# Weight buffers spaced by 64 bytes, one pair of x tiles shifted by 32, and a single mask tile in a hybrid attention layer

## The chip, the cores and the metric

The kernel runs on one core of one Trainium2 chip. The metric is the device time of one execution in microseconds. The unchanged kernel takes 2168.59 us (median of two runs, 2168.49 and 2168.7).

## What is computed

The reference is one decoder layer on 2048 tokens of width 1024, with 16 learned meta tokens ahead of them. Everything is float32. The input is normalised, multiplied by one wide matrix, and the product is cut into ten pieces:

```python
xn = rms_norm(h, norm_gain[l])
proj = xn @ w_in[l]
sb_q, sb_k, sb_v, sw_q, sw_k, sw_v, sb_z, sw_z, g_sb, g_sw = jnp.split(proj, offsets, axis=-1)
o_sb = stick_breaking_attention(sb_q, sb_k, sb_v, valid)            # 8 heads of 64, causal
o_sw = sliding_window_sink_attention(rope(sw_q), rope(sw_k), sw_v, attn_sinks[l], valid)
                                                                    # 16 heads, 2 kv heads, window 128
y_sb = (o_sb * jax.nn.silu(sb_z)) @ w_branch_sb[l]
y_sw = (o_sw * jax.nn.silu(sw_z)) @ w_branch_swa[l]
merged = jax.nn.sigmoid(g_sb) * y_sb + jax.nn.sigmoid(g_sw) * y_sw
h = h + merged @ w_out[l]
return rms_norm(h, final_norm_gain)[:, BLOCK:]
```

## The kernel before

Nearly all arithmetic is matrix products on TensorE. To keep float32 accuracy in the faster float32r format, every operand is split into a high and a low part (`wh`, `wl` for weights, `xh`, `xl` for activations), and a product is three matmuls: high by high, high weights by low activations, low weights by high activations. The first operand below, `lhsT`, is the weight tile of 128x128 that is loaded into the array; the second, `rhs`, is the moving tile of 128x512 that is streamed through it. Lines 403 to 405 are the projection loop, run for each column tile of `w_in` and each of four groups of 512 tokens:

```python
for k in range(KT):                                                     # KT = 8
    T.matmul(acc, lhsT=wh[:, k, :], rhs=xh[g][:, k, :], ...)            # L403
    T.matmul(acc, lhsT=wh[:, k, :], rhs=xl[g][:, k, :], ...)            # L404
    T.matmul(acc, lhsT=wl[:, k, :], rhs=xh[g][:, k, :], ...)            # L405
```

While one matmul streams, the weights of the next one are loaded; a matmul and its weight load are shown apart in the profile (PE and PEld).

The order of the program, in time:

1. A start, in which the first tiles of x are prepared. Here two groups are also multiplied in an unnormalised form, from tiles `uh` and `ul` instead of `xh` and `xl`.
2. Two halves of the sequence, groups 2 and 3 first, then 0 and 1. In each half, projections are woven with sliding-window attention (its matmuls are lines 698, 727, 744), then with stick-breaking attention (lines 841, 863, 889), by a generator that puts a few projection matmuls between pieces of attention. Between and after these come stretches of projections alone, the gate tiles (`gate`, made by `tiles_by_tile`).
3. The end (`finish`): the two branch projections (`project`, lines 223 to 225, with `wh` and `wl` against ring tiles `ringl` or `ringr`) and the output projection (lines 282 to 284, in which `ringl` is loaded as the weights and `ringr` streams).

TensorE's order is written out by hand (`manual_schedule`), so it follows the code; the other engines are ordered by a scheduler, except in the start.

What matters for this change is where tiles lie in a partition of SBUF. `weights` (line 163) takes `wh` and `wl` from pool `w`, three buffers each, 4096 bytes per partition and buffer: 8 blocks of 128 float32. `x_tiles` (line 371) takes pairs `xh`, `xl` of 16384 bytes each from pool `x`, one pair for each of two groups. The ring tiles are 2048 bytes each; two unused tiles, `padl` of 672 bytes (line 189) and `padr` of 1728 bytes (line 243), lie ahead of them. The start addresses in the built program, modulo 512 bytes, are:

| tiles | address modulo 512 |
|---|---|
| `wh`, `wl`, all six buffers | 480 |
| `xh`, `xl`, both pairs | 480 |
| `ringl`, `ringr` | 480 |
| `uh`, `ul` | 320 |

"Distance" in this text is the address of the moving tile of one matmul minus the address of the weights that are loaded while it streams, that is, those of the next matmul, modulo 512. A block of `wh`, `wl`, or of `xh`, `xl`, a ring tile and a slice of 128 columns are all multiples of 512 bytes, so the distance is a property of the pair of tiles: 0 between `xh` or `xl` and any weight buffer, 0 between the ring tiles and the weights and among the ring tiles, 352 between `uh` or `ul` and the weights. Among attention matmuls it takes various values (256 and 384 in line 744, 384 and 448 inside a pair of line 841, 256 and 224 for the low part `wtl` of line 889).

The mask `sel` (line 68) holds two equal copies of a 128x128 pattern, loaded by two DMAs in `late_consts`; line 702 uses it as the predicate of a copy into the scores of two heads.

Of the kernel before, what the change touches and what calls it, by code (L numbers as in the profile page):

```python
# [7 lines left out]
F32 = mybir.dt.float32  # L8
F32R = mybir.dt.float32r
I32 = mybir.dt.int32  # L10
# [6 lines left out]
P = 128  # L17
D = 1024
KT = D // P
# [25 lines left out]
def tile_kernel(ctx, tc, x, xt, meta, metat, gain, w_in, w_sb, w_sw, w_out, sinks, fgain,  # L45
# [6 lines left out]
    V, A, G, T = nc.vector, nc.scalar, nc.gpsimd, nc.tensor  # L52

    def DMA(dst, src):
        nc.sync.dma_start(*(t.bitcast(F32) if t.dtype == F32R else t for t in (dst, src)))

    ctx.enter_context(tc.manual_schedule(engines={mybir.EngineType.PE}))
    cp = ctx.enter_context(tc.tile_pool(name="const", bufs=1, side="left"))
# [3 lines left out]
    def ps(tag):  # L62
        return pp.tile([P, 512], F32, tag=tag, name="ps_" + tag, bufs={"g": 2, "z": 2, "zm": 1, "t": 2, "o": 1}[tag])
# [1 line left out]
    A.preload_act_table_set("natural_log_exp_and_others")  # L65
    ident = cp.tile([P, P], F32, name="ident")
    gn = cp.tile([P, KT], F32, name="gn")
    sel = cp.tile([P, 2, P], I32, name="sel")
    skb = cp.tile([P, 16], F32, name="skb")

    def late_consts():
        for i in range(2):
            DMA(sel[:, i, :], sel_c)
        DMA(skb, sinks.to_broadcast([P, 16]))

    vm = cp.tile([P, 4, 2, P], F32R, name="vm")
# [7 lines left out]
    def dram(name, shape, dt=F32):  # L84
        return dp.tile(shape, dt, tag=name, name=name)
# [16 lines left out]
    def split(h, l, src):  # L102

        if hsplit[0]:
            A.copy(h, src)
        else:
            G.tensor_scalar(h, src, 1.0, 1.0, op0=ALU.mult, op1=ALU.mult)  # L107
        (V if vsplit[0] else G).tensor_tensor(l, src, f32(h), op=ALU.subtract)  # L108
# [44 lines left out]
    wp = ctx.enter_context(tc.tile_pool(name="w", bufs=1, side="right"))  # L153
# [4 lines left out]
    def load(c0, w=w_in):  # L158
        raw = wp.tile([P, KT, P], F32, tag="raw", name="raw", bufs=2)[:, :w.shape[2], :]
        DMA(raw, w[c0 // P])  # L160
        return raw

    def weights(c0, w=w_in, raw=None, split=split):

        if c0 in ready:
            return ready.pop(c0)
        n = w.shape[2]
        wh, wl = (wp.tile([P, KT, P], F32R, tag=t, name=t, bufs=3)[:, :n, :] for t in ("wh", "wl"))
        key = w.name, c0
        if key in kept:  # L170
            for t, k in zip((wh, wl), kept[key]):
                DMA(t, k)
            return wh, wl
        raw = load(c0, w) if raw is None else raw
        split(wh, wl, raw)
        kept[key] = [dram(f"{t}_{w.name}_{c0}", [P, n, P], F32R) for t in "hl"]
        for t, k in zip((wh, wl), kept[key]):
            if put_off is None:
                DMA(k, t)
            else:  # L180
                put_off.append((k, t))
        return wh, wl
# [20 lines left out]
    def finish(ringl, osw, first):  # L203
# [23 lines left out]
        for half, groups in enumerate(halves):  # L227
# [12 lines left out]
            for d, g in order:  # L240
                if d == 4 and g == groups[0]:
                    if half == 0:
                        cp.tile([P, 432], F32, name="padr")
                    osb = {(k, g): gated(od, zs, k, g, ringr, lambda: small("a", AB)) for g in groups for k in range(4)}
                if d not in ws_of:
                    ws_of[d] = first if half == d == 0 else weights(d * P, w_sw)
                ws = ws_of[d]
                acc = bank()
                project(acc, ws, [osw[k, g] for k in range(8)])
                gt = small("gt", 3)  # L250
                DMA(gt, gw[d][g])
                part[d, g] = ringr(F32)
                V.tensor_tensor(part[d, g], acc, gt, op=ALU.mult)
            for d in range(8):
                ws = weights(d * P, w_sb)
                for g in groups:
                    acc = bank()
                    project(acc, ws, [osb[k, g] for k in range(4)])
                    gt = small("gt", 3)
                    DMA(gt, gs[d][g])  # L260
                    V.tensor_tensor(gt, acc, gt, op=ALU.mult)
                    V.tensor_tensor(gt, gt, part[d, g], op=ALU.add)
                    mh, ml = merged[d, g] = ringl(), ringl()
                    A.copy(mh, gt)
                    V.tensor_tensor(ml, gt, f32(mh), op=ALU.subtract)
                out_weights(d, 0)
# [62 lines left out]
    xp = fst.enter_context(tc.tile_pool(name="x", bufs=1, side="right"))  # L329
# [35 lines left out]
    def scale_rows(rs, rb=None):  # L365
# [2 lines left out]
        A.copy(rb, spread(rs, P, 4))  # L368
        return rb

    def x_tiles(key, n):
        xh[key] = xp.tile([P, KT, GT], F32R, tag=f"xh{n}", name="xh")
        xl[key] = xp.tile([P, KT, GT], F32R, tag=f"xl{n}", name="xl")

# [6 lines left out]
    def prep(g, rs):  # L381

        x_tiles(g, g % 2)
        rb = scale_rows(rs)
        for k in range(KT):
            t = ring_x()
            DMA(t, xt[g, k])
            drain(normal(g, k, t, rb))
# [207 lines left out]
    def window(half, groups, sp):  # L596
# [87 lines left out]
        def scores(s, g, i, st):  # L684
            kv = s // 2
            blk = 4 * (g - groups[0]) + i
            sc = sp.tile([P, 4, P + 1], F32, tag="sc", name="sc", bufs=4)
            edge = half == 0 and blk == 7
            if edge:
                G.memset(sc, -1e30)  # L690
            G.tensor_copy(sc[:, :, P], skb[:, 4 * s:4 * s + 4])
            for pr in range(2):
                acc = ps("z")
                av = acc.rearrange("p (a c k) -> p a c k", a=2, c=2)
                for a in range(2):
                    lq = qs[2 * s + pr, g][0][:, a, i * P:(i + 1) * P]
                    for hl in range(2):
                        T.matmul(acc[:, a * 256:(a + 1) * 256], lhsT=lq,
                                 rhs=kk[:, 2 * kv + hl, blk * P:(blk + 2) * P], start=hl == 0, stop=hl == 1)
                nk = NM if edge else P  # L700
                A.copy(sc[:, 2 * pr:2 * pr + 2, :nk], av[:, :, 1, :nk])
                V.copy_predicated(sc[:, 2 * pr:2 * pr + 2, :P], sel, av[:, :, 0, :])
            nm, den = (sp.tile([P, 4], F32, tag=t, name=t, bufs=2) for t in ("nm", "den"))
            V.tensor_reduce(nm, sc, op=ALU.max, axis=AX.X, negate=True)  # L704
            for hh in range(4):
                A.activation(sc[:, hh, :], sc[:, hh, :], AF.Exp, bias=nm[:, hh:hh + 1], accum_out=den[:, hh:hh + 1])  # L706
            V.reciprocal(den, den)
            V.tensor_tensor(sc[:, :, :P], sc[:, :, :P], den.unsqueeze(2).to_broadcast([P, 4, P]), op=ALU.mult)
            st["sc"] = sc
# [49 lines left out]
        def attend():  # L759
            units = [(s, g, i, {}) for s in range(4) for g in groups for i in range(4)]  # L760
            n = len(units)
            for u in range(n + ULAG):
                if u >= ULAG:
                    turn(*units[u - ULAG])
                yield 1.25
                if u < n:
                    last = 2 * units[u][0] + 1, units[u][1]
                    while last not in qs or (clock[0] < qs[last][1] and not ending):
                        yield 0
                    scores(*units[u])  # L770
                    if u < 4:
                        differences(2 * u)
                    yield 0.9
                if u >= ULAG:
                    values(*units[u - ULAG])
# [154 lines left out]
    with (tc.tile_pool(name="start", bufs=1, side="left") as bp,  # L930
# [56 lines left out]
        ready[C_SBK] = weights(C_SBK, raw=raw, split=by_halves)  # L987
        ts = [sbt[0]()]
        x_tiles(("u", g0), 1)
        for k in range(KT):  # L990
            raws.append(bp.tile([P, GT], F32, tag="raw0", name="raw0", bufs=KT))
# [29 lines left out]
        rb0 = scale_rows(rs, bp.tile([P, GT], F32, tag="rb0", name="rb0"))  # L1021
        products(g1, 0, "z")
        x_tiles(g0, 0)
        todo = blocks(g1)
        raw2 = [load(c) for c in (C_SWK, C_SWV)]
# [61 lines left out]
    for half, groups in enumerate(halves):  # L1087
        with tc.tile_pool(name=f"swa{half}", bufs=1, side="left") as sp:
# [8 lines left out]
            if m:  # L1097
                late_consts()
# [29 lines left out]
        with tc.tile_pool(name=f"sb{half}", bufs=1, side="left") as bp:  # L1128
# [9 lines left out]
            if half == 0:  # L1138
                t, u = (bp.tile([P, GT], F32, tag="wh", name="sum", bufs=3)[:, :8] for _ in range(2))
# [77 lines left out]
```

## Time and profile before

| what | value |
|---|---|
| median of the runs | 2168.59 us |
| the profiled execution's own time | 2172.68 us |
| its span, from the first to the last instruction | 2171.0 us |
| mean granted TensorE clock | 0.998 of full speed |
| instructions | 30232 |
| busy: matmul, VectorE, ScalarE, GpSimd | 99%, 63%, 46%, 17% of the span |

The span is one execution on the core. PE is TensorE's matmuls, PEld its weight loads, DVE VectorE, ACT ScalarE, POOL GpSimd, SP the queue that issues the DMAs. A matmul's shown duration is longer than the time until the next one starts, since they are pipelined; the time from start to start is what adds up to the span. The stages are, in us from the span's start: the start to 122, projections with window attention to 375, projections alone to 407, with stick-breaking attention to 752, projections alone to 866, then the second half with window attention to 1128, alone to 1160, stick-breaking to 1665, alone to 1724, and `finish` to the end.

### The profile page before, as it was taken

The page shows a single profiled execution, that of the slowest core. Times are in us where ns is not written, and L with a number is a line of the kernel's source. Part 1 is how long each engine was busy: PE and PEld are TensorE (multiplying, and loading weights), DVE is VectorE, ACT ScalarE, POOL GpSimd, SP SyncE. Part 2 cuts the span into 40 slices and gives each one's busy share as a digit, 9 for nine tenths or more (in the row PEclk, how much of TensorE's full clock was granted, in tenths as well). Part 3 has the DMA queues.
Part 4 walks back from the last instruction along what each step waited for, and adds up shares of the span by engine and source line. Part 5 has one row for each costly group of instructions (what it writes and reads, how often), then busy time and mean ns, then how long its engine had stood idle before and what let it go on. Part 6 is the DMA issues. An engine that isn't in the chain of part 4 may idle for free. (4 is left out here: it accounts for less than half of the span.)

```text
span 2171.0 us, 30232 instructions
## 1 busy us (share of the span) xinstructions
PE 2139.1 (99%) x10614; PEld 1766.3 (81%) x10614; DVE 1358.0 (63%) x2117; ACT 1007.2 (46%) x2328; POOL 372.5 (17%) x486
## 2 busy tenths in 40 slices
PE   8899999999999999999999999999999999999998
PEld 6678888888888888888887888888888888787887
DVE  7787876465555443767746888787775446454453
ACT  6576775344444434777743555555553201221121
POOL 2233343323222300222310000000000232000000
PEclk9999999999999999999999999999999999999999
DMA  9755455755555464444356433333322985468432
GB/s 330 259 182 195 158 189 186 256 194 201 192 180 178 145 212 155 158 160 147 136 170 184 122 112 115 108 98 118 118 88 92 352 310 191 161 226 274 163 108 88
DMA packets 174648, 380.41 MB, mean 175 GB/s; under 512 B 22912, under 2 KB 41088, under 8 KB 174496
## 3 DMA queue, kind: packets, MB, share of 16 engines
q1 hardware_dynamic: 174496, 378.48, 52.0%
q8 instruction: 84, 1.38, 0.3%
q14 instruction: 68, 0.56, 0.1%
HBM read 237.35 MB, written 140.98 MB: 174 GB/s over the span
## 5 line engine op out<-in xcount | busy, mean ns | idle before, releaser
L403 PE MATMUL ps_g<-xh,wh 128*128 128x512 f32 x1544 | 638.3, 413 | 7.2 <-ACT xh L939 6.8
L405 PE MATMUL ps_g<-xh,wl 128*128 128x512 f32 x1544 | 607.7, 394 | 0.6 <-DVE wl L108 0.6
L404 PE MATMUL ps_g<-xl,wh 128*128 128x512 f32 x1544 | 607.8, 394 | 0.0
L852 DVE TENSOR_TENSOR_SCAN row<-row 128x512 f32<-128x512 f32 (+2 forms) x320 | 371.1, 1162 | 168.2 <-POOL row L850 96.7
L405 PEld LDWEIGHTS ps_g<-xh,wl 128*128 128x128 f32 x1544 | 290.9, 188 | 66.4 <-DVE wl L108 1.1
L403 PEld LDWEIGHTS ps_g<-xh,wh 128*128 128x128 f32 x1544 | 292.0, 189 | 54.5 <-ACT xh L939 6.8
L404 PEld LDWEIGHTS ps_g<-xl,wh 128*128 128x128 f32 x1544 | 292.5, 189 | 44.1 <-DVE xl L940 1.3
L845 ACT ACTIVATE row<-ps_z 128x512 f32<-128x512 f32 (+1 forms) x320 | 171.7, 537 | 252.8 <-PE ps_z L841 209.8
L112 DVE SCALAR_TENSOR_TENSOR wtl<-ps_t,wth 128x512 fp32r<-128x512 f32 (+1 forms) x320 | 189.9, 593 | 47.5 <-ACT wth L111 46.0
L111 ACT ACTIVATE wth<-ps_t 128x512 fp32r<-128x512 f32 (+1 forms) x320 | 170.2, 532 | 92.3 <-PE ps_t L863 90.8
L841 PE MATMUL ps_z<-kt,q 128*128 128x512 f32 (+3 forms) x640 | 185.0, 369 | 0.3 <-ACT row L845 0.3
L863 PE MATMUL ps_t<-ident,row 128*128 128x128 f32 x1088 | 171.6, 273 | 1.2 <-DVE row L852 1.2
L863 PEld LDWEIGHTS ps_t<-ident,row 128*128 128x128 f32 x1088 | 135.9, 140 | 37.3 <-DVE row L852 1.7
L850 POOL TENSOR_SCALAR_AFFINE_SELECT row<-row 128x128 f32<-128x128 f32 x128 | 44.8, 351 | 620.0 <-ACT row L845 552.6
L841 PEld LDWEIGHTS ps_z<-kt,q 128*128 128x128 f32 x640 | 118.7, 188 | 26.4 <-ACT row L845 0.8
L889 PE MATMUL ps_o<-wth,vc 128*128 128x512 f32 (+1 forms) x320 | 125.7, 393 | 1.3 <-DVE tmp L894 1.1
L107 POOL TENSOR_SCALAR wh<-raw 128x1024 fp32r<-128x1024 f32 (+1 forms) x63 | 66.9, 1063 | 327.9 <-PE ps_g L404 213.8
L560 ACT ACTIVATE tmp<-ps_g 128x512 f32<-128x512 f32 x112 | 67.0, 598 | 118.6 <-PE ps_g L405 112.6
L889 PE MATMUL ps_o<-wtl,vc 128*128 128x512 f32 (+1 forms) x320 | 116.8, 365 | 0.0
L706 ACT ACTIVATE sc<-sc,nm 128x129 f32<-128x129 f32 x256 | 100.0, 393 | 35.8 <-DVE nm L704 35.1
L108 POOL TENSOR_TENSOR wl<-raw,wh 128x1024 fp32r<-128x1024 f32 (+1 forms) x43 | 95.7, 2226 | 3.1
L621 POOL TENSOR_TENSOR tmp<-tmp 128x512 f32<-128x512 f32 (+1 forms) x37 | 48.7, 1315 | 203.6 <-DVE tmp L620 158.3
(306 smaller groups left out, 3399.3 us busy)
## 6 DMA issues: line engine op xcount, KB each, us to landing
wh<-h_in_w_in SPq DMA_DIRECT2D x66, 512.0 KB, 3.8
wl<-l_in_w_in SPq DMA_DIRECT2D x66, 512.0 KB, 4.8
raw<-in_w_in SPq DMA_DIRECT2D x50, 512.0 KB, 6.0
h_in_w_in<-wh SPq DMA_DIRECT2D x50, 512.0 KB, 3.6
l_in_w_in<-wl SPq DMA_DIRECT2D x50, 512.0 KB, 2.9
q<-qd SPq DMA_DIRECT2D x128, 128.0 KB, 2.9
vc<-vd SPq DMA_DIRECT2D x48, 256.0 KB, 3.1
kd<-tmp SPq DMA_DIRECT2D x32, 256.0 KB, 4.3
```

The costliest lines, as they stand in the source:

```text
L108: (V if vsplit[0] else G).tensor_tensor(l, src, f32(h), op=ALU.subtract)
L111: A.activation(h, acc, AF.Copy, scale=scale)
L112: V.scalar_tensor_tensor(l, acc, scale, f32(h), op0=ALU.mult, op1=ALU.subtract)
L403: T.matmul(acc, lhsT=wh[:, k, :], rhs=xh[g][:, k, :], start=k == 0, stop=False)
L404: T.matmul(acc, lhsT=wh[:, k, :], rhs=xl[g][:, k, :], start=False, stop=False)
L405: T.matmul(acc, lhsT=wl[:, k, :], rhs=xh[g][:, k, :], start=False, stop=k == KT - 1)
L706: A.activation(sc[:, hh, :], sc[:, hh, :], AF.Exp, bias=nm[:, hh:hh + 1], accum_out=den[:, hh:hh + 1])
L841: T.matmul(z[:, :w], lhsT=lq, rhs=kt[h][:, k0:k0 + w], start=t == 0, stop=t == 1)
L845: A.activation(r[:, :w], z[:, :w], AF.Sigmoid, scale=-1.0)
L852: V.tensor_tensor_scan(r[:, :w], r[:, :w], r[:, :w], last[j] if n else 1.0, op0=ALU.mult, op1=ALU.min)
L863: T.transpose(tr[:, j * P:(j + 1) * P], rows_of[h, g, n - (j > i), j][:, k0:k0 + P], ident)
L889: T.matmul(o[:, :n], lhsT=v, rhs=r, start=first and r is wh, stop=last and r is wl)
```

## The change

```diff
-    sel = cp.tile([P, 2, P], I32, name="sel")
+    sel = cp.tile([P, P], I32, name="sel")
...
     def late_consts():
-        for i in range(2):
-            DMA(sel[:, i, :], sel_c)
+        DMA(sel, sel_c)
...
-        wh, wl = (wp.tile([P, KT, P], F32R, tag=t, name=t, bufs=3)[:, :n, :] for t in ("wh", "wl"))
+        wh, wl = (wp.tile([P, KT * P + 16], F32R, tag=t, name=t, bufs=3)[:, :n * P].rearrange("p (k c) -> p k c", c=P) for t in ("wh", "wl"))
...
+    padded = []
+
     def x_tiles(key, n):
+        if n == 0 and not padded:
+            padded.append(1)
+            xp.tile([P, 8], F32, name="padx")
         xh[key] = xp.tile([P, KT, GT], F32R, tag=f"xh{n}", name="xh")
...
-                V.copy_predicated(sc[:, 2 * pr:2 * pr + 2, :P], sel, av[:, :, 0, :])
+                V.copy_predicated(sc[:, 2 * pr:2 * pr + 2, :P], sel.unsqueeze(1).to_broadcast([P, 2, P]), av[:, :, 0, :])
```

Each weight buffer grows from 4096 to 4160 bytes, of which the last 64 are never touched, so that the six buffers start 64 bytes further on from one to the next. A tile of 32 unused bytes is put ahead of one of the two pairs of x tiles. The mask has one copy, read twice by a broadcast access pattern, which frees 512 bytes. Since pool `w` grows downward from the end of memory and the other right-hand pools follow it, the tiles behind it move too. In the built program the addresses modulo 512 become:

| tiles | before | after |
|---|---|---|
| `wh`, three buffers | 480 | 96, 160, 224 |
| `wl`, three buffers | 480 | 288, 352, 416 |
| `xh`, `xl`, two pairs | 480 | 64 and 96 |
| `ringl` | 480 | 480 |
| `ringr` | 480 | 96 |
| `uh`, `ul` | 320 | 320 |

In the projections the distance is now 352, 384, 416, 448, 480 or 0 where `wh` is loaded (two of three matmuls) and 160, 192, 224, 256, 288 or 320 where `wl` is loaded. In `project` it is 256, 320 or 384 (`ringl`) and 384, 448 or 0 (`ringr`) for `wh`, 64, 128 or 192 (`ringl`) and 192, 256 or 320 (`ringr`) for `wl`. In the output projection it is 128 throughout. The distances inside attention that run between tiles of the left-hand pools stay as they are.

The instructions of TensorE, VectorE, ScalarE and GpSimd and their order stay the same; SP issues one DMA less, the second copy of the mask. The lines of the loops above move by a few: 223 to 225 become 222 to 224, 282 to 284 become 281 to 283, 403 to 405 become 407 to 409, and attention's lines move by 4.

## The prediction

> **What bounds the kernel now.** I read the busy times first, then who waited for whom on TensorE, then the order of time inside a long stretch of matmuls. The first line of the page with the engines' busy times, and the two longest waits of the matmuls:
>
> ```profile
> PE 2139.1 (99%) x10614; PEld 1766.3 (81%) x10614; DVE 1358.0 (63%) x2117; ACT 1007.2 (46%) x2328; POOL 372.5 (17%) x486
> ```
> ```profile
> PE ps_g L403 <- ACT xh L939: 6.8, 1, 6.8
> PE ps_zm L528 <- DVE vt L112: 2.7, 2, 1.6
> ```
>
> TensorE works 99% of the span and its two longest waits add to 9.5 us. A busy matmul engine is not yet one at its peak, so the question is how far apart matmuls start. A nanosecond more or less per matmul goes to the end of the program undiminished, with nothing beside it to hide it.
>
> The order of time shows the start to start distance. The columns are the start, the duration, the engine, the line, the tiles. First a stretch of the start in which `xh` and `xl` stream (distance 0 to the weights that are loaded meanwhile), then, six microseconds later, one in which `uh` and `ul` stream (distance 352). First and last of 18 rows each:
>
> ```profile
> 23.16 0.39 PE L403 MATMUL ps_z<-xh,wh 128*128 128x512 f32 x1
> ...
> 27.02 0.39 PE L405 MATMUL ps_z<-xh,wl 128*128 128x512 f32 x1
> ```
> ```profile
> 29.09 0.40 PE L403 MATMUL ps_z<-uh,wh 128*128 128x512 f32 x1
> ...
> 33.06 0.39 PE L405 MATMUL ps_z<-uh,wl 128*128 128x512 f32 x1
> ```
>
> 17 steps take 3.86 us, 227 ns each, at distance 0, and 3.97 us, 233.5 ns each, at distance 352. Shapes, types, PSUM tile and weight pool are the same. The address alone is the likeliest cause of 6.5 ns, and it is what the change touches.
>
> The durations follow the steps, which makes every group's mean usable. The rows below (of one tile's instructions; minimum, median, maximum) give 389 where a step is 227, and 399 and 394 where it averages 233.5, so I take step = duration - 162:
>
> ```profile
> L284 PE MATMUL ps_g<-ringr,ringl x80: 389/389/390, 1857.5 to 2152.4; 128*128 128x512 f32 x80
> L403 PE MATMUL ps_t<-uh,wh x8: 396/399/452, 40.9 to 45.8; 128*128 128x512 f32 x8
> L405 PE MATMUL ps_t<-uh,wl x8: 394/394/402, 41.4 to 46.3; 128*128 128x512 f32 x8
> ```
>
> The table of windows with the instructions of line 404 alone shows the stages (window, its length, PE busy and count, weight loads, clock, DMA): two of projections alone, two with window attention, two with stick-breaking attention.
>
> ```profile
> 752.00:866.00 114.00, 63.49 (x163) 30.61 (x163) 1.00 0.56 187
> 1665.00:1724.00 59.00, 31.91 (x82) 15.39 (x82) 1.00 0.83 302
> 122.00:375.00 253.00, 95.08 (x243) 45.77 (x243) 1.00 0.50 173
> 866.00:1128.00 262.00, 103.00 (x263) 49.53 (x263) 1.00 0.45 153
> 407.00:752.00 345.00, 130.06 (x329) 62.44 (x329) 1.00 0.55 182
> 1160.00:1665.00 505.00, 118.50 (x301) 57.02 (x301) 1.00 0.34 107
> ```
>
> The means are 389.5 and 389.1, then 391.3 and 391.6, then 395.3 and 393.7 ns. So at distance 0 a long run of projections settles at 389, and a run that attention breaks up after three matmuls does not: it pays 231 to 233 ns a step although its distance is 0. Where it settles shows in the order of time at the end of the first window-attention stage, where projections begin again:
>
> ```profile
> 371.68 0.39 PE L403 MATMUL ps_g<-xh,wh 128*128 128x512 f32 x1
> ...
> 373.76 0.39 PE L403 MATMUL ps_g<-xh,wh 128*128 128x512 f32 x1
> ...
> 375.12 0.39 PE L403 MATMUL ps_g<-xh,wh 128*128 128x512 f32 x1
> ```
>
> The first nine steps take 2.08 us, 231 each, the next six 1.36 us, 227 each. Distance 0 has a settled state that is reached after some nine matmuls; that state is what the kernel can lose.
>
> **The change, part by part.** *The settled state.* At the new distances the nearest rows are 352 (settled, 233.5) and the attention matmuls, which run at most a few in a row, at 256, 384 and 224:
>
> ```profile
> L744 PE MATMUL ps_o<-pl,vv x64: 388/393/504, 136.8 to 1128.4; 128*128 128x512 f32 x64
> L744 PE MATMUL ps_o<-ch,xs x64: 389/393/398, 137.1 to 1128.6; 128*128 128x512 f32 x64
> L889 PE MATMUL ps_o<-wtl,vc 128*128 128x512 f32 x224 | 88.2, 394 | 0.0
> ```
>
> They lie at 393 to 394, a step of 231 to 232. From below the bound is the least of these, 388, a step of 226: one nanosecond under distance 0. From above it is 399, the worst place of the 352 pattern, a step of 237. I take 394, +5 ns on a settled step of 389: three rows at three distances lie at 393 or 394, and the 352 pattern as a whole, with 6.5, is not far above.
>
> How many steps are settled: in `finish`, 768 + 384 = 1152 of lines 223 to 225 and 768 of lines 282 to 284, 1920 in all, of which 80 keep distance 0: 1840 x 5 ns = 9.2 us. In the four stretches of projections alone, line 404 counts 163 + 82 in the rows above and 46 + 44 in the two shorter ones of the same table,
>
> ```profile
> 375.00:407.00 32.00, 17.57 (x46) 8.45 (x45) 1.00 0.99 329
> 1128.00:1160.00 32.00, 16.85 (x44) 8.07 (x43) 1.00 0.83 238
> ```
>
> 335 in all and three lines each, 1005; a tenth of these pairs of buffers still has distance 0, so 905 x 5 = 4.5 us. In the two window-attention stages 506 x 3 = 1518 steps stand at 391.5 on the mean, as if half were settled; they go to 394 too, 2.5 ns x 1518 x 0.9 = 3.4 us.
>
> *The unsettled steps.* In the two stick-breaking stages line 404 is at 393.7 to 395.3 with distance 0, and line 889 at 394 with distance 256 and 224. There is nothing to lose or gain: 0, with -6 and +4 ns as the bounds (389 and 399) on 630 x 3 = 1890 steps.
>
> The rule that speaks against all of this is in the Trainium skill, "SBUF — State Buffer", section "Who interferes with whom": the moving operand and the weight load have a read port each, independent of one another, so where the two tiles lie would not matter, and the sum would be 0 in place of 17 us. The trace disagrees: 227 against 233.5 ns in the rows above.
>
> *The mask.* 128 predicated copies read the mask through a broadcast pattern. The trace has them with the plain mask, and it has a broadcast operand in line 708 beside a plain product of the same size in line 562:
>
> ```profile
> L702 DVE COPY_PREDICATED sc<-sel,ps_z x128: 421/445/462, 115.6 to 1111.8; 128x256 f32<-128x256 int32 x128
> L708 DVE TENSOR_TENSOR sc<-sc,den 128x512 f32<-128x512 f32 x64 | 48.6, 759 | 2.0
> L562 DVE TENSOR_TENSOR tmp<-ps_g,tmp 128x512 f32<-128x512 f32 x48 | 32.9, 686 | 67.6 <-ACT tmp L560 57.8 <-DMA kt<-kd 9.7
> 122.00:375.00 253.00, 250.75 (x1341) 209.29 (x1340) 196.55 (x373) 174.02 (x506) 92.55 (x128) 1.00 0.50 173
> 866.00:1128.00 262.00, 259.95 (x1332) 216.74 (x1331) 183.15 (x360) 184.31 (x517) 69.97 (x106) 1.00 0.45 153
> ```
>
> At the ratio 759/686 the copies would take 0.49 us, 6 us more on VectorE over two stages. In them (last two rows; PE, PEld, DVE) VectorE works 197 of 253 and 183 of 262 us, so it has 56 and 79 us of cover, and TensorE hardly waits. Price 0; without cover, 6 us. The dropped DMA is one of the two in
>
> ```profile
> L55 SPq DMA_DIRECT2D sel<-in_sel x2: 429/440/450, 14.0 to 14.5; - x2
> ```
>
> and frees SP's queue for 0.44 us at 14 us, a hundred microseconds before the mask is first read: 0, and -0.4 from below. The 64 unused bytes, and the 32, cost no instruction, and no row of a DMA gets longer.
>
> The sum is 9.2 + 4.5 + 3.4 = 17.1 us. The profiled execution took 2172.7 us (span 2171.0), 4.1 above the median of the runs; it would become 2189.8, and the median 2168.6 + 17.1 = 2185.7, say 2186 us.
>
> **Rivals.** *The distance does nothing*, and `uh` is slow because ScalarE and VectorE write it meanwhile. Time 2168.6. For it: the writes of `uh` and `ul` last to 29.4 us, into that stretch. Against it: line 403 still has its median of 399 ns from 40.9 to 45.8 us. The rule of the Trainium skill named above would give the same.
>
> *Another distance settles sooner or lower (not slower than before).* The mechanism: two streams of reads slip against each other until they find a phase, at distance 0 after nine steps; at another distance the phase is found in one or two. Then the steps in the stick-breaking stages drop from 394.5 to 389, 1890 x 5.5 = 10.4 us, and the settled ones by the 1 ns of the lowest row, 2.8 us: 2168.6 - 13.2 = 2155. It decides where runs of three no longer pay 231 ns. For it: minima of 388 at distances 256 and 384. Against it: medians there of 393.
>
> *Every distance is as bad as the worst place of the 352 pattern.* All go to 399: 2745 x 10 = 27.5 us, 1518 x 7.5 x 0.9 = 10.2, 1890 x 4.5 x 0.9 = 7.7, together 45: 2214. For it: the one settled pattern at a non-zero distance contains it. Against it: only one of three matmuls there.
>
> *The mask does more than 6 us.* If the broadcast doubled the copy, 128 x 0.445 = 57 us on VectorE in two stages with 56 and 79 us of cover; by chance of place perhaps 10 us reach TensorE: 2196 with the rest.
>
> **How the numbers follow.** The forecast, the distances cost 3 to 6.5 ns per settled step, gets 0.69; nothing 0.11; sooner or lower 0.12; all at the worst 0.05; the mask 0.03. The forecast's own range is 2168.6 + 3/5 x 17 = 2179 to 2168.6 + 6.5/5 x 17 = 2191. For 8 in 10 I reach to 2162, half-way into the rival below, and to 2203, between 2191 and the worst. A change of 2% is 43 us, about what a measurement of this kernel can tell from none: slower by more needs the worst at nearly every distance (0.05), faster by more is outside every row (0.01), within 2% has 0.94.
>
> **What would show it.** Right: lines 281 to 283 (distance 128 alone) rise from 389 to about 394; line 408 in the projection stretches too; line 408 in the stick-breaking stages stays at 394; TensorE's busy time grows by about as much as the span, and its longest waits stay those shown. Wrong: 281 to 283 at 389 with the span unchanged (distance does nothing), line 408 under 391 in the stick-breaking stages (it settles sooner), any of these at 399 or more, or a VectorE wait of TensorE in the window-attention stages (the mask). Steps that differ between the six buffers by several nanoseconds would show that each distance has its own price, and that one value for all of them was the weak point of the sum.

## The result and the profile after

The changed kernel takes 2183.84 us (median of two runs, 2183.09 and 2184.58) against 2168.59 us before, a ratio of 1.0068 with a 95% interval of 1.0052 to 1.0085. That is 15.2 us more (11 to 18 by the interval) where 17.1 were summed and 2186 forecast, well inside 2%, but clear of noise.

The engines' busy times of the profiled execution after the change:

```profile
span 2181.4 us, 30231 instructions
PE 2153.7 (99%) x10614; PEld 1766.0 (81%) x10614; DVE 1358.3 (62%) x2117; ACT 1008.6 (46%) x2328; POOL 372.2 (17%) x486
```

TensorE gained 14.6 us of busy time with the same number of matmuls; no other engine moved by more than two. The longest waits of TensorE are those of before:

```profile
PE ps_g L407 <- ACT xh L943: 7.0, 1, 7.0
PE ps_zm L532 <- DVE vt L111: 2.9, 2, 1.6
```

The rows of the output projection (distance 128 now, minimum/median/maximum duration), which stood at 389/389/390:

```profile
L281 PE MATMUL ps_g<-ringr,ringl x80: 390/393/404, 1865.6 to 2162.0; 128*128 128x512 f32 x80
L282 PE MATMUL ps_g<-ringr,ringl x80: 390/393/404, 1865.8 to 2162.2; 128*128 128x512 f32 x80
L283 PE MATMUL ps_g<-ringr,ringl x80: 390/393/404, 1866.0 to 2162.5; 128*128 128x512 f32 x80
```

And the windows of line 408 (404 before) by itself: first two stages of projections alone, then two with window attention, then two with stick-breaking attention. The columns are those of the table before: the window, its length, PE busy and count, weight loads, clock, DMA. The stage limits are shifted by the microseconds that the program runs later:

```profile
755.00:871.00 116.00, 64.19 (x164) 30.80 (x164) 1.00 0.55 185
1671.00:1730.00 59.00, 31.48 (x81) 15.01 (x80) 1.00 0.84 306
122.00:376.00 254.00, 95.69 (x243) 45.67 (x243) 1.00 0.49 172
871.00:1134.00 263.00, 102.79 (x262) 49.22 (x262) 1.00 0.45 152
409.00:755.00 346.00, 130.26 (x331) 62.70 (x331) 1.00 0.54 180
1166.00:1671.00 505.00, 118.82 (x302) 57.20 (x302) 1.00 0.34 107
```

Busy time over count is 391.4 and 388.6 in the stretches alone, 393.8 and 392.3 with window attention, 393.5 and 393.4 with stick-breaking attention. A matmul cut by a window's edge counts whole but adds only a part; counted by whole matmuls the stretches alone stand at 393.0 and 392.7, against 389.5 and 389.1 before. One line of three says little where the steps in a block of three differ, so I compared start to start times of the same matmul in both traces. The table has all steps between two 512-wide matmuls that differ by less than 60 ns between the two, which leaves out the waits of either:

| stage | steps | mean change | sum | predicted |
|---|---|---|---|---|
| start | 369 | +2.2 ns | +0.8 us | not priced |
| with window attention | 1618 | +1.7 ns | +2.8 us | +3.4 us |
| projections alone | 1016 | +4.8 ns | +4.8 us | +4.5 us |
| with stick-breaking attention | 2290 | -0.2 ns | -0.4 us | 0 |
| `finish` | 1889 | +5.2 ns | +9.8 us | +9.2 us |

They sum to 17.8 us. The two profiled executions are only 10.4 us apart (2172.68 and 2183.09), since the one of before had stalls that the other did not: the steps left out of the table are 7.7 us longer in it, 5.3 of them in `finish` and 1.8 in the start. Windows of TensorE in `finish` before the change show the largest:

```profile
1852.00:1950.00 98.00, 96.86 (x423) 1.00 0.52 177
1950.00:1968.00 18.00, 15.93 (x63) 0.95 0.94 326
1966.20:1969.40 3.20, 3.20 (x9) 0.50 0.90 302
```

In 18 us TensorE worked 15.93 us: it waited for data, and for some 3 us after that its matmuls started 430 ns apart, at a granted clock of 0.50. Such stalls come and go between executions (the profile of the run with one pair of x tiles shifted, below, has one like it in `finish`, that of the run with only the mask has none), so a single profile of before is a base to no better than some microseconds. The medians are the better base.

### The profile page after: what moved, and what is told of

It reads as the page before. It is cut to its first block, busy times and chain, and to the rows that moved or that the text cites. A ratio compares the mean times of both kernels' runs of the same rounds, so it can differ in the third digit from the quotient of the medians.

```text
span 2181.4 us, 30231 instructions
## 1 busy us (share of the span) xinstructions
PE 2153.7 (99%) x10614; PEld 1766.0 (81%) x10614; DVE 1358.3 (62%) x2117; ACT 1008.6 (46%) x2328; POOL 372.2 (17%) x486
## 4 chain that ended last, share of the span: by engine, by line
PE 91%; DVE 2%; issue 2%; ACT 2%; DMA 1%; POOL 1%; SPq 0%; ACTq 0%; POOLq 0%; DVEq 0%
PE ps_g L407 15%; PE ps_g L408 15%; PE ps_g L409 15%; PE ps_o L893 6%; PE ps_z L845 6%; PE ps_t L867 5%; PE ps_z L702 3%; PE ps_o L748 2%; PE ps_g L223 1%; PE ps_g L224 1%; PE ps_z L224 1%; PE ps_z L223 1%; PE ps_g L222 1%; PE ps_z L222 1%; PE ps_t L223 1%
```

## The experiments

All but the first keep the single mask copy, so their base is the first. Each time is a median and stands against the median of the kernel before in the same session. "Settled" means the mean step between starts after ten 512-wide matmuls in a row at one distance; it is counted from the start times in the trace.

**Only the mask.**

```diff
-    sel = cp.tile([P, 2, P], I32, name="sel")
+    sel = cp.tile([P, P], I32, name="sel")
...
-        for i in range(2):
-            DMA(sel[:, i, :], sel_c)
+        DMA(sel, sel_c)
...
-                V.copy_predicated(sc[:, 2 * pr:2 * pr + 2, :P], sel, av[:, :, 0, :])
+                V.copy_predicated(sc[:, 2 * pr:2 * pr + 2, :P], sel.unsqueeze(1).to_broadcast([P, 2, P]), av[:, :, 0, :])
```

> Only the mask is changed: one copy, read by a broadcast pattern, one DMA less. All distances of projections and of the end stay 0. If the distance is what costs (theory), the time stays that of before, 2168.6 within 2 us, and the output projection's matmuls stay at a duration of 389 ns. If the mask is what costs (rival), the 15 us of the change appear here, about 2184, and TensorE waits for VectorE in the window-attention stages.

2168.3 against 2168.0, ratio 1.0004 (0.9994 to 1.0013). The mask costs nothing that can be told from noise. In the changed kernel the copy with the broadcast mask takes as long as before (median 445 then):

```profile
L706 DVE COPY_PREDICATED sc<-sel,ps_z x128: 426/446/460, 114.5 to 1115.6; 128x256 f32<-128x256 int32 x128
```

**The spacing without the shift of x.** The change without its `padx` tile.

```diff
-        wh, wl = (wp.tile([P, KT, P], F32R, tag=t, name=t, bufs=3)[:, :n, :] for t in ("wh", "wl"))
+        wh, wl = (wp.tile([P, KT * P + 16], F32R, tag=t, name=t, bufs=3)[:, :n * P].rearrange("p (k c) -> p k c", c=P) for t in ("wh", "wl"))
```

> The mask and the 64-byte spacing of the weight buffers, without the shift of one pair of x tiles. In the projections no buffer pair has distance 0 for all three matmuls of a block, and the end has the same distances as in the changed kernel. Theory (every step at a distance other than 0 loses its settled 227 ns): as the changed kernel, 2181 to 2186. Rival (the shift of the x pair carries a good part): clearly between, 2172 to 2179.

2182.15 against 2168.0, ratio 1.0066 (1.0051 to 1.0081): the spacing alone does nearly all of it, as the theory had it.

**One pair of x tiles shifted, without the spacing.**

```diff
+    padded = []
...
+        if n == 0 and not padded:
+            padded.append(1)
+            xp.tile([P, 8], F32, name="padx")
```

> The mask and the 32-byte shift of one pair of x tiles, without the spacing of weights. One pair has distance 0 to all weights, the other 480; the end stays at 0. Theory: the projections lose half of what they lose in the changed kernel (4.8 us in the stretches alone and 2.8 us with window attention), so 3.8 us: 2171 to 2174, with durations of 389 ns left in the end. Rival (the distances must be many or change from matmul to matmul to cost): 2168.6, since each pair here has one distance only.

2174.18 against 2168.0, ratio 1.0027 (1.0017 to 1.0036). The direction is the theory's, the size is 6.2 us and not 3.8. Distance 480 settles at 233.3 ns (414 steps), +6.7 and not the +4.8 that I had averaged from the changed kernel: the stretches alone gain 3.4 ns on 1008 steps and the stages with window attention 1.5 ns on 1518, together 5.8 us. The rival, that a single constant distance costs nothing, is out.

**Everything moved by 128 bytes.** A pad at the end of the weight pool moves weights, x and `ringr`, a smaller `padl` moves `ringl`.

```diff
+        if not spaced:
+            wp.tile([P, 32], F32, name="padw")
+            spaced.append(1)
...
-        lp.tile([P, 168], F32, name="padl")
+        lp.tile([P, 136], F32, name="padl")
```

> The mask, and every weight buffer, x tile and ring tile moved by the same 128 bytes, to 352 modulo 512: addresses are other ones, all distances stay 0. Theory (the distance counts, not the address): 2168.6 within 2 us, steps settle at 227 ns (duration 389). Rival (the address itself, 480 modulo 512, is what was good): all settled steps are lost, 2180 to 2186.

2166.51 against 2168.0, ratio 0.9995 (0.9986 to 1.0005). The output projection, at other addresses but distance 0, in the view of one tile's instructions:

```profile
L284 PE MATMUL ps_g<-ringr,ringl x80: 389/389/389, 1855.1 to 2146.3; 128*128 128x512 f32 x80
```

A move of all of them by 128 bytes does not matter; how they lie to one another does.

**Two maps of constant distances.** High and low part of a weight get the same address modulo 512, in three places 128 bytes apart; the pairs of x tiles stand 64 apart. In the second map both pairs stand 32 bytes further on.

```diff
+        b = len(spaced) % 3
+        if 0 < len(spaced) < 3:
+            wp.tile([P, 32], F32, name=f"padw{b}")
+        wh, wl = (wp.tile([P, KT, P], F32R, tag=f"{t}{b}", name=t, bufs=1)[:, :n, :] for t in ("wh", "wl"))
+        spaced.append(1)
...
+        if n == 0 and not padded:
+            padded.append(1)
+            xp.tile([P, 16], F32, name="padx")
```

> The mask, and buffers of weights laid so that a high and a low part have the same address modulo 512, at three places 128 bytes apart, with the two pairs of x tiles 64 apart. Each column tile then runs at one constant distance, one of 0, 192, 256, 320, 384, 448; in the end 0, 128, 256 and 384, and 256 in the output projection. Theory: only the tiles at distance 0 settle at a step of 227 ns; the others stand at 230 to 235, each distance with its own value; a sixth of the gate tiles and a third of the branch projections keep distance 0, so the time is 2178 to 2183. Rival (only a change of distance from matmul to matmul keeps a run from settling): every tile settles at 227, time 2168.6.

> The same with both pairs of x tiles 32 bytes further on: constant distances 160, 224, 288, 352, 416 and 480 in the projections, none at 0. Theory: no tile settles at 227 ns, 352 stands at 233, the time is 1 to 2 us above that of the first map, 2179 to 2185. Rival (constant distances settle): 2168.6.

The first map takes 2175.26 against 2168.41, ratio 1.0031 (1.002 to 1.0041), less than the theory allowed; the second 2181.12, ratio 1.0057 (1.0041 to 1.0073), as expected. The reason for the first stands in its output projection, at distance 256 throughout:

```profile
L285 PE MATMUL ps_g<-ringr,ringl x80: 389/389/389, 1862.4 to 2154.3; 128*128 128x512 f32 x80
L286 PE MATMUL ps_g<-ringr,ringl x80: 389/389/389, 1862.6 to 2154.6; 128*128 128x512 f32 x80
L287 PE MATMUL ps_g<-ringr,ringl x80: 388/389/389, 1862.8 to 2154.8; 128*128 128x512 f32 x80
```

256 is as good as 0. With the two runs below ("ring by 32" and "ring by 64"), all the settled steps fall into pairs 256 bytes apart (in brackets: steps counted, and the run):

| distance | settled step, ns | the same + 256 | settled step, ns |
|---|---|---|---|
| 0 | 226.67 (3012, before) | 256 | 226.66 (1116, first map) |
| 32 | 233.35 (735, ring by 32) | 288 | 233.29 (133, second map) |
| 64 | 228.88 (733, ring by 64) | 320 | 228.74 (137, first map) |
| 96 | 233.33 (12, second map) | 352 | 233.37 (155, second map) |
| 128 | 232.35 (170, first map) | 384 | 232.44 (211, first map) |
| 160 | 234.37 (113, second map) | 416 | 234.31 (111, second map) |
| 192 | 233.36 (113, first map) | 448 | 233.32 (723, ring by 64) |
| 224 | 233.31 (102, second map) | 480 | 233.32 (730, ring by 32) |

**The end alone at another distance.** `padl` becomes 176 or 184 floats, so that `ringl` moves by 32 or 64 bytes.

```diff
-        lp.tile([P, 168], F32, name="padl")
+        lp.tile([P, 176], F32, name="padl")
```

> The mask, and in the end alone the ring of the left pool moved by 32 bytes: distance 32 in two thirds of the branch projections, 0 in the rest, 480 in the output projection. The projections before it stay at 0. Theory: 1536 steps of the end lose 3 to 6 ns each, 5 to 9 us: 2173 to 2178, and the stages before the end do not change. Rival (one constant distance settles at 227): 2168.6.

> The same with 64 bytes: distance 64 in two thirds of the branch projections, 448 in the output projection. Theory: again 3 to 6 ns on 1536 steps, 2173 to 2178, with another value for the step than at 32 and 480. Rival (a constant distance settles at 227): 2168.6. If instead a distance of one 64-byte line were free and only odd multiples of 32 cost, this one would stay at 2168.6 and the one at 32 not.

2176.59 and 2173.93 against 2168.41, ratios 1.0043 (1.003 to 1.0056) and 1.0024 (1.0014 to 1.0034). Branch and output projection with 32 bytes (distances 32 and 480), then with 64 (64 and 448):

```profile
L223 PE MATMUL ps_z<-ringl,wh x80: 393/395/397, 1725.6 to 2022.2; 128*128 128x512 f32 x80
L282 PE MATMUL ps_g<-ringr,ringl x80: 395/396/396, 1858.8 to 2155.4; 128*128 128x512 f32 x80
```
```profile
L223 PE MATMUL ps_z<-ringl,wh x80: 388/390/394, 1725.9 to 2021.9; 128*128 128x512 f32 x80
L282 PE MATMUL ps_g<-ringr,ringl x80: 393/396/398, 1857.4 to 2154.8; 128*128 128x512 f32 x80
```

Each distance has a price of its own: 64 costs 2 ns, and 448, as far in the other direction, nearly 7. The price holds to about half a nanosecond: 128, at 232.4 in the table, settles at 232.9 in the output projection of the changed kernel (730 steps). From the table, 768 x (6.7 + 6.7) ns = 10 us with 32 and 768 x (2.2 + 6.7) ns = 7 us with 64; measured 8.2 and 5.5.

**Low parts off the high parts.** So far distance meant the moving tile against the weights loaded while it streams. Here that distance is 0 or 256 in every projection, but two matmuls of three multiply with weights that lie 32 bytes off their moving tile.

```diff
+        wh = wp.tile([P, KT, P], F32R, tag="wh", name="wh", bufs=3)[:, :n, :]
+        if not spaced:
+            wp.tile([P, 8], F32, name="padw")
+            spaced.append(1)
+        wl = wp.tile([P, KT, P], F32R, tag="wl", name="wl", bufs=3)[:, :n, :]
...
+            xl[key] = x_tile("xl")
+            if first:
+                xp.tile([P, 56], F32, name="padx0")
+            xh[key] = x_tile("xh")
...
```

> The mask, and low parts lying 32 bytes off the high parts (weights and x alike), so that in the projections the moving tile stands at distance 0 or 256 to the weights that are loaded under it, those of the next matmul, but 32 bytes off the weights that it is multiplied with in two of three matmuls. In the branch projections one line of three runs at 480. Theory (it is the next weights that count): the projections settle at 227 ns as before, 371 or so in the stretches alone; only the branch projections lose, up to 1152 steps, so 2171 to 2176. Rival (its own weights count): the projections stand at 230 to 233 and the time is 2178 to 2186.

2181.45 against 2168.35, ratio 1.0066 (1.0049 to 1.0083). The projections do not settle at 227. In order of time, in a stretch alone, first and last of 19 rows:

```profile
805.85 0.39 PE L421 MATMUL ps_g<-xh,wh 128*128 128x512 f32 x1
...
810.01 0.39 PE L421 MATMUL ps_g<-xh,wh 128*128 128x512 f32 x1
```

18 steps in 4.16 us, 231.1 ns, which is 680 + 13.3 ns for a block of three matmuls. Over all settled blocks of the projections the mean is 696, since other stretches settle at 697. So the theory falls in this form: the next weights alone are not what counts, and the rival's numbers hold. But its own weights alone are not it either. In the branch projections of the same run only line 228 is off its own weights and only line 227 off the next, yet two of the three lines are slow, and not the one that the rival names:

```profile
L226 PE MATMUL ps_t<-ringl,wh x80: 395/395/395, 1737.3 to 2033.2; 128*128 128x512 f32 x80
L227 PE MATMUL ps_t<-ringl,wh x80: 400/400/400, 1737.5 to 2033.4; 128*128 128x512 f32 x80
L228 PE MATMUL ps_t<-ringl,wl x80: 389/389/389, 1737.8 to 2033.7; 128*128 128x512 f32 x80
```

Their steps (233, 239 and 228 ns) sum to 700, 20 above 680. One tile out of line costs the neighbours too. The theory as mended: all tiles of a block must lie at the same address modulo 256, and one that does not slows the rest as well. That it does so by moving their phase is a picture that no run shows.

**Only the low parts of x off.** The same with the weights left in line.

```diff
+            xl[key] = x_tile("xl")
+            if first:
+                xp.tile([P, 8], F32, name="padx0")
+            xh[key] = x_tile("xh")
...
```

> The mask, and only the low parts of x moved, by 32 bytes against everything else in the projections: one matmul of three has its moving tile off, by the same 32 bytes against the weights that it is multiplied with and against those loaded under it. The end stays at 0. Theory, as mended after the run with the low parts moved: an offset anywhere in the block of three costs, and costs more than that one matmul's 6.7 ns, since a change from matmul to matmul moves the phase too; 10 to 20 ns a block, so 680 blocks settled now lose 7 to 13 us: 2174 to 2181. Rival (each matmul pays for its own offset alone): 6.7 ns a block on some 650 settled blocks, 4.3 us: 2172 to 2173.

2175.93 against 2168.01, ratio 1.0036 (1.0022 to 1.0049), inside the mended theory's range and above the rival's. One matmul of three is off. First and last of 19 rows in a stretch alone, then the same in a later one:

```profile
805.87 0.40 PE L417 MATMUL ps_g<-xh,wh 128*128 128x512 f32 x1
...
810.07 0.40 PE L417 MATMUL ps_g<-xh,wh 128*128 128x512 f32 x1
```
```profile
1690.19 0.39 PE L417 MATMUL ps_g<-xh,wh 128*128 128x512 f32 x1
...
1694.35 0.39 PE L417 MATMUL ps_g<-xh,wh 128*128 128x512 f32 x1
```

18 steps in 4.20 us, 233.3 ns, are 700 for a block, as bad as if all three were off by 32. But that is one stretch of the four: the later one takes 4.16 us, 231.1 ns, 693 for a block, as the run above did at 806 us. So one layout can settle in more than one way, and a single stretch does not give its price. Over all settled blocks both runs stand at the same 696 ns: one tile of three out of line costs as much as two, some 16 ns a block.

**Distances that are no multiples of 32.** High and low part share a buffer here, read from offsets of 0, 8 or 16 bytes.

```diff
+        o = (0, 2, 4)[b]
+        t = wp.tile([P, 2 * KT * P + (8 if b else 0)], F32R, tag=f"whl{b}", name="wh", bufs=1)
...
+        o = 4 if n else 0
+        t = xp.tile([P, 2 * KT * GT + 2 * o], F32R, tag=f"x{n}", name="xh")
```

> The mask, and distances that are no multiples of 32: 0, 504, 496, 488, 464 and 448 in the projections, one for each column tile, high and low parts in one buffer; in the branch projections 0, 504 and 464, in the output projection 0. If reads are served in pieces of 16 bytes or more, 504 (8 bytes short of a multiple of 256) still behaves as 0, a step of 227, or as its neighbour at 480, 233. If a distance exists at which the two reads never meet, a step below 226.67 ns appears here, the only place where it still could. Theory as it stands: all but 0 lie between 227 and 235, the time at 2172 to 2178; rival (finer distances find a free phase): under 2168.

2177.24 against 2168.35, ratio 1.004 (1.0025 to 1.0055). Settled means: 504 at 230.7 ns, 496 at 233.1, 488 at 228.1, 464 at 233.3, 448 at 228.4. Eight bytes already cost 4 ns, and no distance lies below that of 0. That 448 is at 228.4 here and at 233.3 in the table means that where the tiles lie counts as well: here both stand 16 bytes off a multiple of 32, there on one. How it counts was not tried.

**Attention's tiles in line too.** In the stick-breaking stages nearly every 512-wide matmul then has distance 0 or 256 to the next weights.

```diff
-                kt[h] = bp.tile([P, (4 - groups[0]) * GT + NM], F32R, tag="k", name="kt", bufs=2)
+                if not kt:
+                    bp.tile([P, 40], F32, name="padk")
+                kt[h] = bp.tile([P, (4 - groups[0]) * GT + NM + 48], F32R, tag="k", name="kt", bufs=2)
```

> The mask, and the tiles of the stick-breaking stage in the left pool moved so that every pair of moving tile and next weights there, attention's too, has distance 0 modulo 256; all else as before. Theory (a run needs some nine matmuls to settle, and transposes break it up after three to six): the 1890 projection steps there stay at 231 to 232 ns, time 2166 to 2169. Rival (attention's own distances keep the run from settling): the projections and attention's 512-wide matmuls there go toward 227, 5 to 9 us less, 2159 to 2164, a version that beats both kernels.

2167.01 against 2168.01, ratio 0.9995 (0.9986 to 1.0004): no gain that can be told from noise. The mean step there goes from 231.75 to 231.02 ns over 1899 steps, 1.4 us. Where that little comes from shows in one run of 17 matmuls, its tenth and its last, with the mask alone and then with attention in line:

```profile
542.33 0.40 PE L402 MATMUL ps_g<-xh,wh 128*128 128x512 f32 x1
...
543.95 0.39 PE L404 MATMUL ps_g<-xh,wl 128*128 128x512 f32 x1
```
```profile
544.94 0.39 PE L402 MATMUL ps_g<-xh,wh 128*128 128x512 f32 x1
...
546.53 0.39 PE L404 MATMUL ps_g<-xh,wl 128*128 128x512 f32 x1
```

The seven steps take 1.62 us, 231 each, and 1.59 us, 227 each. Over both stages the steps from the tenth on go from 231.9 to 226.8, so attention's own distances did keep long runs from settling. But only 39 of the 515 runs between narrower matmuls, transposes above all, are longer than ten, and the first nine steps stay at 231.4 (231.7 with the mask alone). So most runs there are too short to settle at any distance. No kernel here beats both by more than a measurement can tell.

## Why the prediction was right, point by point

**The settled state is what was lost.** Shown: the stages in which it was found before (`finish`, the stretches alone, half of the steps with window attention) carry 17.4 of the 17.8 us, and the stick-breaking ones, in which it is hardly reached, carry nothing. The sign named for it came: lines 281 to 283 rose from 389 to 393, line 408 in the stretches alone too. The run with everything moved and the one with the mask alone take away the other candidates.

**+5 ns a settled step.** It measured +4.8 and +5.2. That is a mean over prices that differ: 64 alone costs 2 ns, 0 and 256 nothing, the rest 6 to 8. That the one value agrees with this mean is luck. It came from short runs in attention, at 256, 384 and 224; that they were unsettled, not typical of their distance, did not show since unsettled steps average 231 to 232 at any distance. At 256 alone the choice would have been wrong: it settles at 226.66. The prediction itself named one value for all distances as its weak point.

**The stages with window attention.** 3.4 was summed, 2.8 came. "As if half were settled" was near enough: of 1518 such steps before, 42% take 228 ns or less.

**The stick-breaking stages at 0.** Right, and in the main for the reason given: the runs are too short. The run with attention's tiles in line adds that the few long ones were held up by attention's own distances.

**The mask at 0.** Right: the copy did not become slower at all, so the 6 us of VectorE time that the broadcast was to cost, taken from line 708, were not there to be covered.

**The rivals.** *The distance does nothing* is out by the changed kernel and nine runs, all clear of noise, and with it what the prediction drew from the rule of the Trainium skill, "SBUF — State Buffer", "Who interferes with whom", that the place of the two tiles would not matter: 226.7 against 233.3 ns settled, at 0 and at 32 bytes. Where the traces and the page differ, the traces decide. *Another distance settles sooner or lower*: no distance tried settles below 226.6, and the stick-breaking stages stayed at 231 to 232. *Every distance at the worst place*: the highest settled mean is 234.4, not 237.

**What was wrong in it.** The start was not priced (+0.8 us). The settled state does not always take some nine matmuls: three to ten steps pass, as the last section shows. A nanosecond per matmul was to go to the end "undiminished". It does not quite: in the changed kernel and the nine runs with an offset the summed steps come to some 118 us and the times to 99, less in every one. Against the profile of the run with only the mask, the steps next to a wait or a transpose are 0.9 us shorter with window attention and 1.3 in `finish`, so a part is hidden there. The three terms measured 17.4 us where 17.1 were summed, and this made 15.2 of them. Distance was defined modulo 512 and against the next weights alone; the table has a period of 256, and the run with the low parts off the high ones shows that neither the next weights nor a matmul's own decide alone. In the changed kernel both views give offsets nearly everywhere, so the sum did not depend on it. Which reads meet, if it is reads that meet, and why blocks of one layout settle at 13, 17 or 20 ns above 680, stays open.

## What to carry to other kernels

Where TensorE works 99% of the span, look at the time from start to start: 227 against 233 ns decided this kernel, and no wait and no engine's share showed it (a matmul's duration did, by the same few nanoseconds). In long runs of float32r matmuls, lay weight and moving tiles, high and low parts alike, at the same address modulo 256 bytes, and count the bytes of any pad before adding it. Measure a layout over all stretches, not one: the same tiles settled in more than one way. The gain is only there where a run is long enough to settle, up to some ten matmuls here; between pieces of attention it was worth 1.4 us of steps, which no time showed.

## What the runs showed of the hardware that was not expected

The addresses of weights and moving tiles in SBUF, taken against one another, change the rate of matmuls, with a period of 256 bytes: settled steps of 226.7 ns at 0 and 256, 228.8 at 64 and 320, 232.4 at 128 and 384, 233.3 to 234.4 at the others on a grid of 32. An offset of 8 bytes costs 4 ns. After an interruption three to ten steps pass before the good phase is found. In the trace before, the steps from 880.9 us, behind the scores of line 698, are 229, 234, 235, 225, 230, 235, 230, 232, 231 ns and then 227. Nearly the same values come after other interruptions, begun at a later place: from 789.1 us 233, 236, 224, 231, 236, 228, 233, 231, then 227. From 214.1 us, again behind line 698, three steps are enough. A tile that is out of line makes its neighbours slower as well, while a matmul's own step can stay near 228. With one tile of three out of line, a block settles at 693 ns in some stretches of one execution and at 700 in another.
